# Attention of the second block: one wide row of scores per tile of queries, with one maximum and one exponential

## The chip, the cores and the metric

The kernel runs on one core of one Trainium2 chip. The metric is the device time of one execution in microseconds (us), as the median of the runs shown. The engines are named as the profile names them: PE (matmul; PEld is its weight load), DVE (vector), ACT (scalar), POOL (GpSimd) and SP (which issues DMAs). PSUM is the accumulator memory that PE writes and that DVE and ACT read; it has eight banks of 512 float32 columns.

## The reference, cut to what matters

The program is two blocks, one behind the other. The first is a mixer with a mixture of experts; the second has two layers, and each layer has, beside other branches, an attention of 4 query heads over 2 key heads of width 64. Only the softmax part of this attention is touched:

```python
def one_block(qi):
    sc = jnp.einsum('bqkgd,bskd->bkgqs', qi, k_all, preferred_element_type=jnp.float32)
    p = jax.nn.softmax(sc, axis=-1).astype(v_all.dtype)
    return jnp.einsum('bkgqs,bskd->bqkgd', p, v_all)
```

`k_all` and `v_all` are 256 context tokens and then 1024 latent tokens, so that a row of scores for a latent query has 1280 columns. In the first of the two layers the 256 context queries attend too, to the 256 context tokens alone; in the second layer only the latent queries do.

## The kernel before

The touched code stands in `layer(l)`, which is called twice, for layer 0 and layer 1. By the time it runs, queries and keys lie transposed in SBUF (`qst`, `kst`), values in `vst`. One **job** is one head and 256 queries, that is, two tiles of 128 queries (`qi` = 0 and 1). Layer 0 has 20 jobs (four of them context queries with 256 columns instead of 1280), layer 1 has 16.

Each job has two parts, which are generators:

- `weights(hd, q0, ...)` makes the softmax weights. For each tile of queries PE writes scores in blocks of up to 512 columns (`s`, L1595, two matmuls for each block: high and low part of the keys), each block in a bank of its own out of five. DVE takes a maximum of each block (L1596), then the maximum of those (L1598) and scales it (L1599). ACT takes the exponential of each block into the SBUF tile `E` and sums each (L1601; the sum's read-out is a second row, ACTIVATION_READ_ACCUMULATOR). DVE adds the three sums (L1603) and inverts (L1604); POOL makes a diagonal matrix `dg` of the inverse (L1606).
- `values(hd, q0, ...)` uses them. PE puts the row sums' inverses into the PSUM bank `o` (L1616), transposes `E` in groups of four 128x128 pieces into one of two banks `t` (L1621). Each `t` is split into a high part `et0` and a low part `et1`: three of five by ACT and DVE (L141, L142), two of five by an ACT copy `er` (L1629) and two POOL operations (L1630, L1631). PE multiplies both with the values into `o` (L1637). At the end ACT copies a part of `o` (`pvl`, L1644), DVE adds it and multiplies the gate (`oa`, `gr`, L1645, L1647), POOL finishes (L1648). There is one bank `o`.

PSUM is full: five banks `s`, two `t`, one `o`. The loop at the end of the code interleaves the values of one job with the weights of the next. The final order on each engine is not that of the code: a scheduler sorts the instructions when the program is built, and a tile pool puts a wait before an instruction that overwrites what another engine still reads. Each engine then runs its queue strictly in order.

Of the kernel before, what the change touches and what calls it, by code (L numbers as in the profile page):

```python
# [10 lines left out]
F32 = mybir.dt.float32  # L11
# [3 lines left out]
AF = mybir.ActivationFunctionType  # L15
OP = mybir.AluOpType
AX = mybir.AxisListType
# [3 lines left out]
P = 128  # L21
D = 1024
T = 1024
C = 256
N = T + C
# [97 lines left out]
def build(ctx, tc, A, out):  # L123
# [6 lines left out]
    V, S, G, PE, SY = nc.vector, nc.scalar, nc.gpsimd, nc.tensor, nc.sync  # L130
# [18 lines left out]
    def bank(pool, tag, bufs):  # L149
        return lambda: pool.tile([P, 512], F32, name=tag, tag=tag, bufs=bufs)  # L150

    ident = load(const, A["k_ident"], [P, P], "ident")
# [251 lines left out]
    with ExitStack() as es:  # L404
# [4 lines left out]
        for j in range(4):  # L409
            s = gemv_chunk(pools, A["w_mod"][0], lh, 512 * j)  # L410
            to_columns(pools, s, mod1[:, 4 * j:4 * j + 4, :], col["b_mod"][:, 4 * j:4 * j + 4])
        V.scalar_tensor_tensor(sc1, mod1[:, 8:16, :], 1.0, col["norm1"][:, :, None].to_broadcast([P, 8, 2]),
                               op0=OP.add, op1=OP.mult)
    with ExitStack() as es:
# [4 lines left out]
        ps = es.enter_context(tile_pool(name="ps1", bufs=1, space=PSUM))  # L419
# [57 lines left out]
        for f2 in range(4):  # L477
            wt = wstream(wp, win, 704 + 256 * f2)
            for f in (2 * f2, 2 * f2 + 1):
# [13 lines left out]
                for a, b in ((0, C), (C, N)):  # L493
                    for j in (0, 1, 3, 4):
# [3 lines left out]
                                               op0=OP.mult, op1=OP.add)  # L498
# [75 lines left out]
    with ExitStack() as es:  # L574
        gp = es.enter_context(tile_pool(name="mg", bufs=1, reuse_waits="tile"))
        ps = es.enter_context(tile_pool(name="ps2", bufs=1, space=PSUM))
# [17 lines left out]
        bias = load(gp, A["b_gate"][0].rearrange("(g o) -> g o", o=1), [16, 1], "bias")  # L594
# [50 lines left out]
        for h in range(4):  # L645
            f0, b0 = 10 * h, 64 + 10 * h
            V.tensor_tensor_scan(R[:, 2, f0:f0 + 10], R[:, 0, f0:f0 + 10], R[:, 1, f0:f0 + 10], 0.0,
                                 op0=OP.max, op1=OP.add)
            V.tensor_tensor_scan(R[:, 2, b0 + 1:b0 - 1:-1], R[:, 0, b0 + 1:b0 - 1:-1], R[:, 1, b0 + 1:b0 - 1:-1], 0.0,
                                 op0=OP.max, op1=OP.add)  # L650
# [629 lines left out]
    def layer(l):  # L1280
# [295 lines left out]
        with ExitStack() as es:  # L1576
            ap = es.enter_context(tile_pool(name="ab", bufs=1, side="right", reuse_waits="tile"))
            ps = es.enter_context(tile_pool(name="ps9", bufs=1, space=PSUM, reuse_waits="tile"))
            pt_, po_ = bank(ps, "t", 2), bank(ps, "o", 1)
            def weights(hd, q0, Es, dgs):  # L1580

                kh = hd // 2
                nk = C if q0 < C else N
                kbs = [(k0, min(512, nk - k0)) for k0 in range(0, nk, 512)]
                nb = len(kbs)
                for qi in range(2):
                    sl = slice(q0 + qi * P, q0 + qi * P + P)
                    E = ap.tile([P, N], F32, name="E", bufs=5)
                    mx = ap.tile([P, 4], F32, name="mx", bufs=4)
                    dn = ap.tile([P, 4], F32, name="dn", bufs=4)  # L1590
                    sb = []
                    for b, (k0, n) in enumerate(kbs):
                        sc = ps.tile([P, 512], F32, name="s", tag="s", bufs=5)
                        for x in range(2):
                            PE.matmul(sc[:, :n], qst[:, hd, sl], kst[x][:, kh, k0:k0 + n], start=x == 0, stop=x == 1)  # L1595
                        V.tensor_reduce(mx[:, b:b + 1], sc[:, :n], axis=AX.X, op=OP.max)  # L1596
                        sb.append(sc)
                    V.tensor_reduce(mx[:, 3:4], mx[:, 0:nb], axis=AX.X, op=OP.max)  # L1598
                    V.tensor_scalar(mx[:, 3:4], mx[:, 3:4], -0.125, None, op0=OP.mult)  # L1599
                    for b, (k0, n) in enumerate(kbs):  # L1600
                        S.activation(E[:, k0:k0 + n], sb[b][:, :n], AF.Exp, scale=0.125, bias=mx[:, 3:4],  # L1601
                                     accum_out=dn[:, b:b + 1])
                    V.tensor_reduce(dn[:, 3:4], dn[:, 0:nb], axis=AX.X, op=OP.add)  # L1603
                    V.reciprocal(dn[:, 3:4], dn[:, 3:4])  # L1604
                    dg = ap.tile([P, P], F32, name="dg", bufs=4)
                    G.tensor_scalar(dg, ident, dn[:, 3:4], 1.0, op0=OP.mult, op1=OP.mult)  # L1606
                    Es.append(E)
                    dgs.append(dg)
                    yield
# [158 lines left out]
```

## Time and profile before

| | us |
|---|---|
| median of 3 runs (lowest to highest) | 3309.79 (3307.93 to 3311.59) |
| the profiled execution | 3317.06 |
| its span, first to last instruction | 3315.2 |
| attention of layer 0 in that span, about | 2492 to 2648 |
| attention of layer 1 in that span, about | 3084 to 3221 |
| busy over the span: PE, DVE, ACT, POOL | 3116.6, 2218.9, 1536.9, 642.6 |

The profile names each instruction by its engine, its line and its tiles (`out<-in`). "Busy" of PE has the end of a matmul modelled, so a row of n matmuls is longer than n times their distance; the chain view gives the distance. The granted clock is the share of TensorE's full clock that the chip allowed.

### The profile page before, as it was taken

To read this page: it belongs to the slowest core of one execution; us is meant where nothing else is said; L and a number is where in the kernel's file an instruction comes from. 1 tells how busy PE (TensorE), PEld (TensorE's weight loads), DVE (VectorE), ACT (ScalarE), POOL (GpSimd) and SP (SyncE) were. 2 spreads that over 40 slices of the span, in tenths; PEclk is the share of its full clock that TensorE was granted. 3 is DMA by queue.
4 is the path that set the end of the run, shared out by engine and by line. 5 is a ranking of instruction groups with operands and counts; after the bars stand their busy time and mean duration, and the time that the engine had idled before them with its cause. 6 is when DMAs were issued, how large, how long until landed. Compare 5 with 4: busy or idle time off the path is not lost. (4 is left out here: it accounts for less than half of the span.)

```text
span 3315.2 us, 47729 instructions
## 1 busy us (share of the span) xinstructions
PE 3116.6 (94%) x17089; PEld 2623.6 (79%) x17089; DVE 2218.9 (67%) x4837; ACT 1536.9 (46%) x3076; POOL 642.6 (19%) x852
## 2 busy tenths in 40 slices
PE   7997998999999999959999999899999898999999
PEld 5985876999998888858887777688877787887787
DVE  4485878667666653488999888677427746642773
ACT  4223444555555222217777677621137714212770
POOL 0012322222222000330110010211014501101450
PEclk9998999999999999979999999899999999999999
DMA  8541111000003532459999997433200033111002
GB/s 291 151 121 42 37 43 64 7 15 10 5 11 101 153 113 67 166 205 340 393 386 376 359 355 263 154 109 109 65 29 33 20 123 124 45 48 47 33 28 100
DMA packets 224010, 425.93 MB, mean 128 GB/s; under 512 B 28684, under 2 KB 121468, under 8 KB 223772
## 3 DMA queue, kind: packets, MB, share of 16 engines
q1 hardware_dynamic: 215708, 393.51, 33.7%
q0 software_dynamic: 8064, 29.36, 3.1%
q8 instruction: 135, 2.21, 0.3%
q14 instruction: 103, 0.84, 0.1%
HBM read 379.22 MB, written 43.61 MB: 128 GB/s over the span
## 5 line engine op out<-in xcount | busy, mean ns | idle before, releaser
L145 PE MATMUL acc<-hH,wHL 128*128 128x512 f32 (+1 forms) x1296 | 485.4, 376 | 6.1 <-ACT wHL L141 4.1
L146 PE MATMUL acc<-hL,wHL 128*128 128x512 f32 (+1 forms) x1296 | 483.9, 374 | 0.5 <-DVE hL L142 0.5
L147 PE MATMUL acc<-hH,wHL 128*128 128x512 f32 (+1 forms) x1296 | 482.1, 373 | 0.0
L142 DVE TENSOR_TENSOR ewL<-ewr,ewH 128x1024 fp32r<-128x1024 f32 x320 | 371.7, 1221 | 17.0 <-ACT ewH L141 13.9
L141 ACT ACTIVATE ewH<-ewr 128x1024 fp32r<-128x1024 f32 x320 | 328.5, 1059 | 80.4 <-PE acc L1217 69.4
L145 PEld LDWEIGHTS acc<-hH,wHL 128*128 128x128 f32 x1296 | 244.3, 189 | 55.3 <-ACT wHL L141 7.1
L146 PEld LDWEIGHTS acc<-hL,wHL 128*128 128x128 f32 x1296 | 244.5, 189 | 44.9 <-issue 2.6
L147 PEld LDWEIGHTS acc<-hH,wHL 128*128 128x128 f32 x1296 | 243.9, 189 | 44.3 <-issue 1.6
L142 DVE TENSOR_TENSOR wHL<-wr,wHL 128x512 fp32r<-128x512 f32 (+1 forms) x160 | 111.9, 704 | 224.4 <-ACT wHL L141 223.6
L142 DVE TENSOR_TENSOR et<-t,et 128x512 fp32r<-128x512 f32 x264 | 180.1, 686 | 60.6 <-ACT et L141 59.2
L141 ACT ACTIVATE wHL<-wr 128x512 fp32r<-128x512 f32 (+1 forms) x160 | 101.6, 638 | 254.0 <-PE acc L146 221.6
L141 ACT ACTIVATE et<-t 128x512 fp32r<-128x512 f32 x264 | 156.5, 606 | 133.7 <-PE t L917 113.2
L1217 PE MATMUL acc<-ewH,xTH 128*128 128x512 f32 x512 | 201.7, 394 | 0.2 <-ACT xTH L141 0.2
L1217 PE MATMUL acc<-ewH,xTL 128*128 128x512 f32 x512 | 200.8, 392 | 0.0
L302 DVE SCALAR_TENSOR_TENSOR ga<-gw,lh,ga 128x512 f32<-128x512 f32 x224 | 161.0, 749 | 52.2 <-DMA gw<-in_w_mod_dram 51.0
L183 POOL TENSOR_SCALAR E<-E,sm 128x512 f32<-128x512 f32 (+1 forms) x192 | 117.6, 630 | 326.2 <-ACT E L172 101.2
L1217 PE MATMUL acc<-ewL,xTH 128*128 128x512 f32 x512 | 161.5, 399 | 13.8 <-DVE ewL L142 13.8
L170 DVE TENSOR_REDUCE sm<-s 128x1 f32<-128x512 f32 (+1 forms) x192 | 113.1, 598 | 59.3 <-PE s L901 54.6
L145 PE MATMUL acc<-wHL,hH 128*128 128x256 f32 (+1 forms) x464 | 144.9, 321 | 2.9 <-DVE hH L430 1.3
L146 PE MATMUL acc<-wHL,hH 128*128 128x256 f32 (+1 forms) x464 | 139.8, 307 | 0.0
L1596 DVE TENSOR_REDUCE mx<-s 128x1 f32<-128x512 f32 (+1 forms) x200 | 114.8, 589 | 28.7 <-PE s L1595 27.0
L147 PE MATMUL acc<-wHL,hL 128*128 128x256 f32 (+1 forms) x464 | 130.6, 317 | 2.7 <-DVE hL L1315 2.2
(568 smaller groups left out, 7864.9 us busy)
## 6 DMA issues: line engine op xcount, KB each, us to landing
ewr<-in_w_e_up_dram SPq DMA_DIRECT2D x64, 1024.0 KB
ewr<-in_w_e_gate_dram SPq DMA_DIRECT2D x62, 1024.0 KB
wr<-in_w_in_dram SPq DMA_DIRECT2D x152, 256.0 KB
ewr<-in_w_e_down_dram SPq DMA_DIRECT2D x34, 1024.0 KB
ahead<-in_w_e_down_dram SPq DMA_DIRECT2D x30, 1024.0 KB
gw<-in_w_mod_dram SPq DMA_DIRECT2D x96, 256.0 KB
gw<-in_w_mod_dram SPq DMA_DIRECT2D x32, 512.0 KB
wm<-in_w_mod_dram SPq DMA_DIRECT2D x4, 2048.0 KB
```

The lines of the kernel that those rows point to most:

```text
L141: S.activation(H, src, AF.Copy)
L142: V.tensor_sub(L, src, H)
L145: PE.matmul(o, lh[0], rh[0], start=start, stop=False)
L146: PE.matmul(o, lh[0], rh[1], start=False, stop=False)
L147: PE.matmul(o, lh[1], rh[0], start=False, stop=stop)
L170: V.tensor_reduce(ng[:, b:b + 1], sc, axis=AX.X, op=OP.max)
L183: G.tensor_scalar(E[:, k0:k0 + n], E[:, k0:k0 + n], f[:, b:b + 1], 1.0, op0=OP.mult, op1=OP.mult)
L302: V.scalar_tensor_tensor(acc[x], wk, ck, acc[x], op0=OP.mult, op1=OP.add) if k else
L1217: PE.matmul(pa[:, n], x[:, k], w[:, 512 * n:512 * n + 512], start=k == 0 and x is xT[0] and w is H, stop=k == 7 and w is L)
L1596: V.tensor_reduce(mx[:, b:b + 1], sc[:, :n], axis=AX.X, op=OP.max)
```

## The change

The five banks `s` become one tile `wide_s` of 2 x 1280 columns. The scores of the first query tile of a job lie in columns 0 to 1279 of it (two banks and the first half of the third), those of the second in columns 1280 to 2559 (the second half of the third bank and two more). The matmuls are the same in number and size; the second tile's blocks are now 256, 512, 512 wide, so that none crosses a bank. One maximum and one exponential run over all 1280 columns. The maxima over the three maxima (L1598) and the sum over the three sums (L1603) go. For a context tile the first 256 columns of its half are used.

```diff
--- before.py
+++ after.py
@@ -1577,33 +1577,32 @@
             ap = es.enter_context(tile_pool(name="ab", bufs=1, side="right", reuse_waits="tile"))
             ps = es.enter_context(tile_pool(name="ps9", bufs=1, space=PSUM, reuse_waits="tile"))
             pt_, po_ = bank(ps, "t", 2), bank(ps, "o", 1)
+            wide_s = ps.tile([P, 2, N], F32, name="s", tag="s", bufs=1)
+            wide_s = (wide_s[:, 0], wide_s[:, 1])
+
             def weights(hd, q0, Es, dgs):
 
                 kh = hd // 2
                 nk = C if q0 < C else N
-                kbs = [(k0, min(512, nk - k0)) for k0 in range(0, nk, 512)]
-                nb = len(kbs)
                 for qi in range(2):
                     sl = slice(q0 + qi * P, q0 + qi * P + P)
                     E = ap.tile([P, N], F32, name="E", bufs=5)
-                    mx = ap.tile([P, 4], F32, name="mx", bufs=4)
-                    dn = ap.tile([P, 4], F32, name="dn", bufs=4)
-                    sb = []
-                    for b, (k0, n) in enumerate(kbs):
-                        sc = ps.tile([P, 512], F32, name="s", tag="s", bufs=5)
+                    mx = ap.tile([P, 2], F32, name="mx", bufs=4)
+
+                    if nk == N:
+                        sc = wide_s[qi]
+                        kbs = ((0, 512), (512, 512), (1024, 256)) if qi == 0 else ((0, 256), (256, 512), (768, 512))
+                    else:
+                        sc, kbs = wide_s[qi][:, :C], ((0, C),)
+                    for k0, n in kbs:
                         for x in range(2):
-                            PE.matmul(sc[:, :n], qst[:, hd, sl], kst[x][:, kh, k0:k0 + n], start=x == 0, stop=x == 1)
-                        V.tensor_reduce(mx[:, b:b + 1], sc[:, :n], axis=AX.X, op=OP.max)
-                        sb.append(sc)
-                    V.tensor_reduce(mx[:, 3:4], mx[:, 0:nb], axis=AX.X, op=OP.max)
-                    V.tensor_scalar(mx[:, 3:4], mx[:, 3:4], -0.125, None, op0=OP.mult)
-                    for b, (k0, n) in enumerate(kbs):
-                        S.activation(E[:, k0:k0 + n], sb[b][:, :n], AF.Exp, scale=0.125, bias=mx[:, 3:4],
-                                     accum_out=dn[:, b:b + 1])
-                    V.tensor_reduce(dn[:, 3:4], dn[:, 0:nb], axis=AX.X, op=OP.add)
-                    V.reciprocal(dn[:, 3:4], dn[:, 3:4])
+                            PE.matmul(sc[:, k0:k0 + n], qst[:, hd, sl], kst[x][:, kh, k0:k0 + n], start=x == 0, stop=x == 1)
+                    V.tensor_reduce(mx[:, 0:1], sc, axis=AX.X, op=OP.max)
+                    V.tensor_scalar(mx[:, 0:1], mx[:, 0:1], -0.125, None, op0=OP.mult)
+                    S.activation(E[:, :nk], sc, AF.Exp, scale=0.125, bias=mx[:, 0:1], accum_out=mx[:, 1:2])
+                    V.reciprocal(mx[:, 1:2], mx[:, 1:2])
                     dg = ap.tile([P, P], F32, name="dg", bufs=4)
-                    G.tensor_scalar(dg, ident, dn[:, 3:4], 1.0, op0=OP.mult, op1=OP.mult)
+                    G.tensor_scalar(dg, ident, mx[:, 1:2], 1.0, op0=OP.mult, op1=OP.mult)
                     Es.append(E)
                     dgs.append(dg)
                     yield
```

In the built program the change moves instructions on every engine in both attention stages. In the rows below a name's number tells buffers apart, and `[waits ...]` names the engines whose progress the instruction waits for.

PE before, within the second layer: `s_31075`, `s_31079` and `s_31083` are the three blocks of one query tile, `s_31118` the first block of the next tile, `o`/`et`/`t` belong to the values of earlier jobs.

```order
L1595 MATMUL s_31075<-kst0_28961,qst_28958 128x512 [waits Activation_49]
L1595 MATMUL s_31075<-kst1_28962,qst_28958 128x512
L1637 MATMUL o_30887<-et1_30937,vst_28963 128x256 [waits Pool_49]
...
L1595 MATMUL s_31079<-kst0_28961,qst_28958 128x512 [waits Activation_49]
L1595 MATMUL s_31079<-kst1_28962,qst_28958 128x512
L1621 MATMUL t_31044<-ident_68,E_30863 128x128 [waits Activation_49]
...
L1595 MATMUL s_31083<-kst0_28961,qst_28958 128x256 [waits Activation_49]
L1595 MATMUL s_31083<-kst1_28962,qst_28958 128x256
L1595 MATMUL s_31118<-kst0_28961,qst_28958 128x512 [waits Activation_49]
```

PE now, at a like place: `s_28952` is the wide tile; here its first half is written for the next job. `E_29511` and `E_29584` are the weights of the two query tiles of the job before, `t_29634` the first bank of their transposes. (The rows left out repeat the two above them.)

```order
L1615 MATMUL o_29631<-dg_29523,ones_28608 128x128 [waits DVE_49,Activation_49]
L1599 MATMUL s_28952<-kst0_28610,qst_28607 128x512 [waits Activation_49]
L1599 MATMUL s_28952<-kst1_28611,qst_28607 128x512
...
L1599 MATMUL s_28952<-kst0_28610,qst_28607 128x256
L1599 MATMUL s_28952<-kst1_28611,qst_28607 128x256
L1620 MATMUL t_29634<-ident_68,E_29584 128x128
L1620 MATMUL t_29634<-ident_68,E_29511 128x128
```

What moved: the blocks of one tile, which stood apart with a wait each, stand in one run behind one wait on ACT; and the transposes that read `E_29584`, the newest exponential, come right behind the run without any wait of their own.

ACT before, in the second layer: three exponentials of one tile follow each other, between the copies of `t` and `pvl`.

```order
L141 ACTIVATE et0_31049<-t_31044 128x512 [waits PE_49,Activation_49]
L1629 ACTIVATE er_31064<-t_31057 128x512 [waits PE_49,Activation_49,Pool_49]
L141 ACTIVATE et0_31101<-t_31096 128x512 [waits PE_49,Activation_49]
L1601 ACTIVATE E_31072,dn_31074<-s_31075,mx_31073 128x512 [waits DVE_49]
L1601 ACTIVATE E_31072,dn_31074<-s_31079,mx_31073 128x512
L1601 ACTIVATE E_31072,dn_31074<-s_31083,mx_31073 128x256
L1644 ACTIVATE pvl_31109<-o_31013 64x256 [waits PE_49]
```

ACT now, one whole job from one second-half exponential (`E_29584`) to the next (`E_29690`), with the first-half one (`E_29617`) between them.

```order
L1602 ACTIVATE E_29584,mx_29585<-s_28952,mx_29585 128x1280 [waits DVE_49]
L141 ACTIVATE et0_29639<-t_29634 128x512 [waits PE_49,Activation_49]
L1628 ACTIVATE er_29654<-t_29647 128x512 [waits PE_49,Activation_49,Pool_49]
L141 ACTIVATE et0_29667<-t_29662 128x512 [waits PE_49,Activation_49]
L1602 ACTIVATE E_29617,mx_29618<-s_28952,mx_29618 128x1280 [waits DVE_49]
L1628 ACTIVATE er_29682<-t_29675 128x512 [waits PE_49,Activation_49,Pool_49]
L141 ACTIVATE et0_29709<-t_29704 128x512 [waits PE_49,Activation_49]
L1643 ACTIVATE pvl_29717<-o_29631 64x256 [waits PE_49]
L1602 ACTIVATE E_29690,mx_29691<-s_28952,mx_29691 128x1280 [waits DVE_49]
```

What moved: one exponential stands for three, and between two of them stand two or three copies of `t`, each of which waits for PE.

DVE now, at the same place: `mx_29618` is the maximum for `E_29617`; `et1_29640` is the low part of `t_29634`.

```order
L1603 RECIPROCAL mx_29585<-mx_29585 128x1 [waits Activation_49]
L1600 TENSOR_REDUCE mx_29618<-s_28952 128x1 [waits PE_49,Pool_49]
L142 TENSOR_TENSOR et1_29640<-t_29634,et0_29639 128x512 [waits Activation_49]
L1601 TENSOR_SCALAR mx_29618<-mx_29618 128x1 [waits DVE_49]
L142 TENSOR_TENSOR et1_29668<-t_29662,et0_29667 128x512 [waits Activation_49]
L1603 RECIPROCAL mx_29618<-mx_29618 128x1 [waits Activation_49]
```

What moved: the one maximum of the tile stands alone, and the scaling that the exponential waits for (L1601 now) has a subtraction between it and the maximum.

## Rows read from the trace of the kernel before

**Rows 1.** The page, part 1: busy time of the engines over the span.

```profile
PE 3116.6 (94%) x17089; PEld 2623.6 (79%) x17089; DVE 2218.9 (67%) x4837; ACT 1536.9 (46%) x3076; POOL 642.6 (19%) x852
```

**Rows 2.** Windows: us, busy time (instructions) of each engine, granted clock, DMA share, GB/s.

```profile
3084.00:3221.00 137.00, 126.91 (x886) 112.54 (x886) 106.43 (x302) 110.85 (x291) 78.83 (x107) 0.98 0.02 8
3100.00:3200.00 100.00, 95.61 (x685) 84.61 (x684) 81.05 (x235) 83.66 (x223) 64.84 (x88) 1.00 0.00 1
```

**Rows 3.** Timeline, ACT's L1644: first and last of 20, then of 16 jobs.

```profile
2506.52 0.38 ACT L1644 ACTIVATE pvl<-o 64x256 f32<-64x256 f32 x1
...
2647.34 0.38 ACT L1644 ACTIVATE pvl<-o 64x256 f32<-64x256 f32 x1 [1.44 <-PE o L1637]
...
3100.30 0.38 ACT L1644 ACTIVATE pvl<-o 64x256 f32<-64x256 f32 x1
...
3220.78 0.38 ACT L1644 ACTIVATE pvl<-o 64x256 f32<-64x256 f32 x1 [1.44 <-PE o L1637]
```

**Rows 4.** Groups by shape, 3084 to 3221 us: busy us, mean ns | idle before.

```profile
L1601 ACT ACTIVATE E<-s,mx 128x512 f32<-128x512 f32 x64 | 43.7, 695 | 5.9 <-DVE mx L1599 5.9
L1596 DVE TENSOR_REDUCE mx<-s 128x1 f32<-128x512 f32 x62 | 41.9, 684 | 3.9 <-PE s L1595 3.3
L1631 POOL TENSOR_TENSOR et<-er,et 128x512 fp32r<-128x512 f32 x30 | 38.5, 1285 | 1.8
...
L142 DVE TENSOR_TENSOR et<-t,et 128x512 fp32r<-128x512 f32 x50 | 34.0, 683 | 3.4 <-ACT et L141 3.0
...
L141 ACT ACTIVATE et<-t 128x512 fp32r<-128x512 f32 x50 | 29.6, 605 | 11.2 <-PE t L1621 10.6
...
L1630 POOL TENSOR_SCALAR et<-er 128x512 fp32r<-128x512 f32 x30 | 18.5, 617 | 17.1 <-ACT er L1629 15.5 <-PE o L1637 0.5 <-PE s L1595 0.4
L1629 ACT ACTIVATE er<-t 128x512 f32<-128x512 f32 x30 | 18.0, 601 | 0.7
L1601 ACT ACTIVATE E<-s,mx 128x256 f32<-128x256 f32 x32 | 15.6, 489 | 0.0
...
L1596 DVE TENSOR_REDUCE mx<-s 128x1 f32<-128x256 f32 x31 | 13.1, 422 | 8.9 <-PE s L1595 8.3
...
L1644 ACT ACTIVATE pvl<-o 64x256 f32<-64x256 f32 x16 | 6.1, 379 | 8.2 <-PE o L1637 8.0
```

**Rows 5.** Chain that ended last, the second layer's attention: start us, us, pieces merged.

```profile
3098.37 1.90 ACT E L1601 x6
...
3103.91 0.87 PE t L1621 x8
...
3106.64 0.84 PE o L1637 x7
3108.16 0.93 PE s L1595 x4
```

**Rows 6.** Timeline, 3126 to 3140 us: start us, us, engine, line [idle <-releaser].

```profile
3128.37 0.14 DVE L1599 TENSOR_SCALAR mx<-mx 128x1 f32<-128x1 f32 x1
...
3128.54 0.69 ACT L1601 ACTIVATE E<-s,mx 128x512 f32<-128x512 f32 x1 [0.57 <-DVE mx L1599]
...
3129.13 0.19 ACT L1601 ACTIVATION_READ_ACCUMULATOR E<-s,mx 128x1 f32 x1
...
3130.73 1.41 PE L1595 MATMUL s<-kst,qst 128*128 128x256 f32 x6
...
3137.99 0.23 ACT L1601 ACTIVATION_READ_ACCUMULATOR E<-s,mx 128x1 f32 x1
...
3138.28 0.50 PE L1595 MATMUL s<-kst,qst 128*128 128x256 f32 x2 [0.17 <-ACT E L1601]
```

**Rows 7.** Line L1243: ns min/median/max of an ACT read across two banks.

```profile
L1243 ACT ACTIVATE ea<-acc x16: 1006/1028/1029, 1510.4 to 2041.8; 128x1024 f32<-128x1024 f32 x16
```

**Rows 8.** Windows with a lower granted clock (the column behind POOL).

```profile
300.00:330.00 30.00, 16.15 (x66) 11.16 (x66) 16.19 (x45) 11.14 (x16) 11.76 (x9) 0.64 0.15 57
2060.00:2100.00 40.00, 26.14 (x103) 20.09 (x101) 23.46 (x28) 17.57 (x24) 3.95 (x5) 0.75 0.43 136
```

## The prediction

> **What bounds the kernel now.** I read the page first, then windows of the touched stages, the last-ending chain in them, their groups by shape and single handovers. PE is busy for 94% of the span [rows 1], so time is saved only where PE waits. The two attention stages are the place to look, since the change touches nothing else. In layer 1's PE is busy 126.9 of 137 us, but ACT 110.9 and DVE 106.4 too [rows 2]: three engines are each near full, and the chain passes from one to another (pieces of PE, ACT and, in between, DVE) [rows 5].
>
> Time per job: the last ACT instruction of a job runs at 3100.30 in the first and at 3220.78 in the last of layer 1's 16 jobs [rows 3]: 120.5 us over 15 steps, **8.03 us a job**. In layer 0, 140.8 us go over 19 steps, three of which end a short context job.
>
> What a job costs PE: transposes stand 0.109 apart (8 in 0.87), value matmuls of 256 columns 0.12 (7 in 0.84), score matmuls of 512 columns 0.2325 (4 in 0.93) [rows 5]. A full job has 20, 20 and 8 of these and 4 score matmuls of 256 columns (0.12 each, as the value matmuls): 2.18 + 2.40 + 1.86 + 0.48 = 6.9; four small ones for the diagonals, taken as transposes, make 7.4. So 0.6 us a job is all that shorter work on ACT and DVE could win: 31 steps of full jobs (15 in layer 1, 16 in layer 0) x 0.6 = 19 us.
>
> **What is removed.** ACT: three exponentials of a tile take 1.90 from the first start to the last sum [rows 5]. One of 512 with its sum takes 0.78 (3128.54 to 3129.32) [rows 6]; columns cost 0.206 us per 256 (695 - 489 ns) [rows 4], so 1280 take 0.78 + 3 x 0.206 = **1.40**. DVE: maxima of 684, 684 and 422 ns [rows 4] become one of 684 + 3 x 262 = 1470 ns, **1.47**. The small reductions over three columns go as well; L1599, of the same size, takes 0.14 [rows 6]. That is 0.5 us of ACT and 0.6 of DVE per tile, twice a job. Does an access over more than one bank cost extra? The nearest row says no: ACT reads 1024 columns in two banks in 1028 ns [rows 7], less than twice one of 512. PE's work and the DMAs stay.
>
> **What is added: a wait.** Before, each block of scores had its own bank of five and waited for the exponential that last read that bank. Now, in PE's order, the six matmuls of a tile stand behind one wait on ACT, and the transposes of the newest weights (`E_29584`) follow without a wait. Since they read what that exponential wrote, the wait ahead of the scores must already cover it. The first tile's scores therefore wait for the second tile's exponential of the job before; and those of the second tile for the first's, by the same pattern. The two halves never work at the same time. They share the third bank, and that is where I see the reason. So scores, maximum, scaling and exponential of each tile form one closed chain through the whole stage.
>
> The chain for one tile: from the sum's end (3137.99 + 0.23) to the scores 0.06; six score matmuls with their end 1.41; maximum 1.47; scaling 0.14 and 0.03 on to ACT [rows 6]; exponential 1.40. Sum 4.51 us, **9.0 us a job**, even if nothing ever stands in its way. That is 1.0 more than now.
>
> Things do stand in its way, since each queue is in order. I follow one job of the commonest pattern from the end of the second tile's exponential (time 0), with the durations of [rows 4] and the distances above, 0.05 for a handover, 0.2 for the last result of PE to land (1.41 against 1.17 of distances), and the next instruction on ACT or DVE starting 0.1 before the last one's reported end, as the sum's row does [rows 6].
>
> - PE: scores 0.06 to 1.23, then six transposes to 1.9. ACT copies `t` 1.8 to 2.4 and `er` 2.3 to 2.9 (605 and 601 ns). The next four transposes wait for `er` (their bank): 2.95 to 3.4.
> - DVE: maximum 1.5 to 3.0; the subtraction that stands before the scaling (683 ns) to 3.6; scaling to 3.65. ACT has one more copy ahead (from those transposes, 3.65 to 4.25), so the first tile's exponential runs 4.15 to 5.55.
> - POOL, from `er`: 617 ns to 3.6, 1285 ns to 4.9. PE needs that low part, so it stands until 4.95, then seven value matmuls (0.84) and four transposes (0.44): the second tile's scores start at 6.25 rather than 5.6, and land at 7.65.
> - ACT: `er` 5.5 to 6.1, POOL's two parts after that to 8.1; PE's last eight value matmuls wait for it and land at 9.2; `pvl` (379 ns) to 9.6. DVE: a subtraction to 7.8, maximum 7.75 to 9.2, scaling 9.3. The second exponential stands behind `pvl`: 9.55 to 10.95.
>
> So about **11.0 us a job** in this pattern. In a second pattern, in which the first tile's exponential stands ahead of that third copy, it runs 3.7 to 5.1, the scores follow at once and land at 6.55; maximum to 8.05, a subtraction ahead of the scaling to 8.75, exponential to **10.3**. In PE's order layer 1 has 13 jobs of the first and 2 of the second kind, layer 0 5 and 10, and one more that I count as the second: 18 x (11.0 - 8.03) + 13 x (10.3 - 8.03) = 53.5 + 29.5 = **+83 us**. The context tiles (8) have the same wait; their blocks are short, and I count nothing for them. Upper bound: all of a chain of half a full tile's, 8 x 1.6 = 13 us. Start and end of the stages hold the same instructions; nothing counted.
>
> The profiled execution took 3317.06, 7.3 above the median of the runs shown (0.22%); the sum is +83 against either, so from the median 3309.8 I get **3393 us**.
>
> **A rule weighed.** The order has the wait ahead of all six matmuls of the first tile, the first four of which write banks that the other half doesn't touch. If only the third bank tied the halves, those four (0.93) [rows 5] could run ahead of the wait in every job: 31 x 0.93 = 29 us less, 3364. The order shows the wait ahead of them, so I go by the order. [...]
>
> **Rivals.**
>
> 1. **The bare chain.** Copies, POOL and PE's other work fall into the gaps better than my pass has them, and only the 9.0 decides: 31 x (9.02 - 8.03) = +31, **3341**. For it: DVE and ACT have 0.6 and 0.5 us a tile less to do. Against it: `pvl` and the copies stand ahead of the exponentials in ACT's order, and wait for PE and POOL.
> 2. **A lower clock on top.** PE works 7.4 of 11 us, in pieces with gaps. [...] At 0.83 PE's 7.4 become 8.9; if half of the 1.5 lies on the path, 31 x 0.75 = +23, **3416**; all of it, 3439. [...]
> 3. **Faster.** The exponential is over before PE gets round to the next scores, so that the wait costs nothing and PE alone is left: 7.4 a job, -19 us, **3290**. It decides if the chain is under 3.7 us a tile (half of 7.4): maximum and exponential together would have to take 2.1 instead of 2.87. No row points there; by columns they don't come below 2.87.
> 4. **No change.** The chain comes out at 4.0 a tile, and shorter work pays for the wait: **3310**. It asks for 0.5 us less than the rows give.
> 5. **Only the third bank waits**, as weighed above: **3364**. Against it is the place of the wait in PE's order.
>
> **How the numbers follow.** From no change a measurement of this kernel tells about 0.2%, 6.6 us. Chances: my pass, with its error of some tenths per job (3370 to 3415), 0.55; bare chain 0.17; only the third bank 0.05; lower clock 0.15; no change 0.03; faster 0.05. Slower by over 0.2%: 0.55 + 0.17 + 0.05 + 0.15 = 0.92. The range reaches from the bare chain, 3338, to the lower clock with part of the context tiles' 13 us, 3430. It leaves out no change, faster, and the tails of the others.
>
> **What would show it.** Right: a step of 10.3 to 11.0 us from `pvl` to `pvl`; one exponential of about 1.3 us plus its sum, one maximum of 1.47; PE waiting on "ACT E" before the scores and on POOL's low part; PE's busy share in the stages well under 90%; the two stages together some 80 us longer, and all else as it was. Wrong: scores of one half overlapping the other half's exponential, or a wide maximum or exponential far from 1.47 and 1.40 (my lines by columns failed), or a step at 8 us or less. A granted clock under 1 in the middle of a stage speaks for the second rival.

## The result and the profile after

The changed kernel takes **3433.0 us** (median of 4 runs, 3426.6 to 3433.5) against 3310.7 for the kernel before (4 runs): ratio 1.0361, 95% interval 1.0349 to 1.0373, slower by 122 us. The forecast was 3393 with a range up to 3430. The sign and the serial chain came as forecast; the size lies 3 us above the range.

The profiled execution has a span of 3431.1 us, 115.9 more than before. The sums below are made against that. Line numbers of the touched part have moved: scores are now L1599, the maximum L1600, its scaling L1601, the exponential L1602, `pvl` L1643. First the page's part 1, to set beside [rows 1]:

```profile
PE 3167.7 (92%) x17089; PEld 2647.0 (77%) x17089; DVE 2206.0 (64%) x4565; ACT 1512.0 (44%) x2820; POOL 644.2 (19%) x852
```

ACT and DVE lose 25 and 13 us of busy time. PE's instructions are as many as before, and yet PE is busy 51 us longer. Most of that is not a lower clock: a job had 95.61 / 100 x 8.03 = 7.7 us of busy PE before, at a clock of 1.00 [rows 2], and has 9.27 in the last single step below, at 1.00 as well; over 31 steps that is 49 us. "Busy" has the end of a matmul modelled, and PE's work now stands in more separate pieces; that this makes up the difference is not shown.

The next lines are from the view of one line, the scores: what PE and its weight load waited for there (us, times), first before, then now.

```profile
its engine sat idle before it (us, times) until:
  ACT E L1601: 15.4, 19
```

```profile
its engine sat idle before it (us, times) until:
  ACT E L1602: 84.9, 72
```

The two queues are counted apart, PE 28 times and its weight load 44 times now, so the 72 is not the number of tiles (of which there happen to be 72 too). PE stands only where it comes to the scores before the exponential is over. That the order holds everywhere is seen from the start times: none of the 400 recorded score matmuls starts while an exponential runs, where 179 of 400 do in the kernel before. The groups by shape in layer 1's attention (busy us, mean ns | idle before) show what became of the rows of [rows 4]:

```profile
L1600 DVE TENSOR_REDUCE mx<-s 128x1 f32<-128x1280 f32 x28 | 41.6, 1487 | 23.0 <-PE s L1599 23.0
...
L1602 ACT ACTIVATE E<-s,mx 128x1280 f32<-128x1280 f32 x29 | 38.4, 1325 | 3.5 <-DVE mx L1601 3.2
...
L1602 ACT ACTIVATION_READ_ACCUMULATOR E<-s,mx 128x1 f32 x29 | 5.7, 197 | 0.0
```

The windows below have the same columns as [rows 2]. The first four run from one `pvl` to the next, so each is a job's step; the fifth is all of layer 1's 15 steps, the last all of layer 0's 19.

```profile
3174.10:3186.90 12.80, 10.60 (x56) 8.69 (x56) 6.16 (x12) 5.95 (x10) 5.24 (x7) 0.87 0.01 1
3186.90:3199.26 12.36, 9.39 (x56) 7.42 (x56) 6.29 (x12) 7.30 (x12) 5.28 (x7) 1.00 0.00 0
3199.26:3208.86 9.60, 8.82 (x56) 7.18 (x56) 5.86 (x10) 4.46 (x8) 5.26 (x7) 1.00 0.01 3
3208.86:3220.20 11.34, 9.27 (x56) 7.33 (x56) 6.34 (x13) 5.88 (x10) 5.25 (x7) 1.00 0.00 0
3162.74:3336.68 173.94, 142.39 (x826) 114.48 (x826) 90.78 (x163) 88.28 (x149) 74.71 (x100) 0.95 0.00 1
...
2503.25:2703.19 199.94, 159.24 (x938) 130.37 (x938) 107.06 (x203) 100.78 (x177) 84.79 (x117) 0.93 0.01 2
```

Where the 115.9 us are: layer 1's steps 173.94 against 120.48 [rows 3], +53.5; layer 0's 199.94 against 140.82, +59.1; the stretch between the stages' `pvl` (2703.19 to 3162.74) +6.6; the first `pvl` comes 3.3 earlier; behind the last one both kernels take 94.4. Of the 6.6, 3.1 lie between layer 1's first scores and its first `pvl` (25.3 against 22.2); the rest lies ahead of those scores, and 2.9 of the 3.3 ahead of layer 0's first scores, in code that the change leaves alone.

One job at full clock, in the timeline, PE, DVE and ACT alone:

```profile
3210.49 0.19 ACT L1602 ACTIVATION_READ_ACCUMULATOR E<-s,mx 128x1 f32 x1
...
3210.73 1.43 PE L1599 MATMUL s<-kst,qst 128*128 128x512 f32 x6
...
3212.00 0.82 PE L1620 MATMUL t<-ident,E 128*128 128x128 f32 x6
3212.27 1.49 DVE L1600 TENSOR_REDUCE mx<-s 128x1 f32<-128x1280 f32 x1 [1.39 <-PE s L1599]
...
3214.27 0.14 DVE L1601 TENSOR_SCALAR mx<-mx 128x1 f32<-128x1 f32 x1
...
3214.97 1.32 ACT L1602 ACTIVATE E<-s,mx 128x1280 f32<-128x1280 f32 x1
...
3215.80 1.10 PE L1636 MATMUL o<-et,vst 128*128 128x256 f32 x7 [0.21 <-POOL et L1630]
...
3217.09 1.41 PE L1599 MATMUL s<-kst,qst 128*128 128x256 f32 x6
...
3218.68 1.48 DVE L1600 TENSOR_REDUCE mx<-s 128x1 f32<-128x1280 f32 x1
...
3220.20 0.38 ACT L1643 ACTIVATE pvl<-o 64x256 f32<-64x256 f32 x1 [2.17 <-PE o L1636]
3220.60 1.33 ACT L1602 ACTIVATE E<-s,mx 128x1280 f32<-128x1280 f32 x1
```

Read it as the closed chain: the sum ends at 3210.68, scores start at 3210.73, the maximum at 3212.27, the exponential at 3214.97. The second tile's scores (3217.09) do not wait for ACT, which was done at 3216.38; PE is late there, since its seven value matmuls stood for POOL until 3215.80. The second exponential stands behind `pvl`. That is the course the forecast walked through.

### The profile page after: what moved, and what is told of

Its sections match the earlier page's. It is cut to its first block, busy times and chain, and to the rows that moved or that the text cites. A ratio compares the mean times of both kernels' runs of the same rounds, so it can differ in the third digit from the quotient of the medians.

```text
span 3431.1 us, 47209 instructions
## 1 busy us (share of the span) xinstructions
PE 3167.7 (92%) x17089; PEld 2647.0 (77%) x17089; DVE 2206.0 (64%) x4565; ACT 1512.0 (44%) x2820; POOL 644.2 (19%) x852
## 5 line engine op out<-in xcount | busy, mean ns | idle before, releaser
L1599 PE MATMUL s<-kst,qst 128*128 128x512 f32 (+1 forms) x400 | 110.5, 417 | 40.5 <-ACT E L1602 36.9
L1636 PE MATMUL o<-et,vst 128*128 128x256 f32 x656 | 128.4, 310 | 14.7 <-POOL et L1630 6.3
```

The source lines that it names most:

```text
L1599: PE.matmul(sc[:, k0:k0 + n], qst[:, hd, sl], kst[x][:, kh, k0:k0 + n], start=x == 0, stop=x == 1)
L1636: PE.matmul(pv[:, :256], vst[:, k, kh, 1 - g:3 - g].rearrange("p b e -> p (b e)"), ET[x][:, kk * 256:kk * 256 + 256], start=(k == 0 and x ...
```

## The experiments

Three theories were put against each other. **T**: the scores of a tile are tied to the tile just before, and that tie makes a serial chain. **W**: a wide maximum and a wide exponential cost it by themselves, because no maximum runs beside scores any more. **C**: PE's gaps bring the granted clock down, on top of either.

### Width against tie, cleanly: three kernels with 1024 keys

With 1024 keys a tile of queries needs two banks, so that two tiles fit beside the transposes' two banks with no bank shared. `k1_1024_keys` is the kernel before with fewer keys. `k2_wide_own_tiles` has the wide operations and a score tile for each half:

```diff
+ wide_s = [ps.tile([P, 1024], F32, name=f"s{x}", tag=f"s{x}", bufs=1) for x in range(2)]
...
+ V.tensor_reduce(mx[:, 0:1], sc, axis=AX.X, op=OP.max)
+ S.activation(E[:, :nk], sc, AF.Exp, scale=0.125, bias=mx[:, 0:1], accum_out=mx[:, 1:2])
```

`k3_wide_one_tile` differs from it in two lines:

```diff
- wide_s = [ps.tile([P, 1024], F32, name=f"s{x}", tag=f"s{x}", bufs=1) for x in range(2)]
+ wide_s = ps.tile([P, 2, 1024], F32, name="s", tag="s", bufs=1)
+ wide_s = (wide_s[:, 0], wide_s[:, 1])
```

> Leaves out the last 256 keys for the latent queries (1024 of 1280 keys: scores, exponentials, transposes, values), so its time is to be compared with the two that leave out the same. Otherwise the kernel before: five banks of scores in turn, a maximum and an exponential per 512 columns. A job is a fifth smaller but for the fixed parts: 8.03 x 0.8 = 6.4 to 6.6 us, 31 x 1.5 = -45: about 3265 (3255 to 3290).

> The same 1024 keys as the run with 1024 keys, with one maximum and one exponential of 1024 columns per tile of queries, each half in a tile of two banks of its own, and the transposes with both their banks. A half's scores wait for that half's exponential of the job before. Theory T (the tie costs it): within -15 to +10 us of the narrow kernel with 1024 keys. Theory W (the width costs it): 30 to 60 us above it.

> As the wide kernel with 1024 keys, but both halves lie in one tile of four banks; no bank is shared, two banks for each half. In PE's order every tile's scores wait for the exponential of the tile just before, as in the changed kernel. Theory T: closed chain per tile 0.06 + 1.15 + 1.23 + 0.2 + 1.2 = 3.85, with the queues' delays as in the changed kernel (11.3 against 9.0 bare) 4.8: 9.6 a job against about 6.5, so +70 to +110 us above the wide kernel with tiles of their own. If the shared third bank, and not the shared tile, is what ties: no more than 10 us above it. Theory W: no more than 10 us above it, since the width is the same.

Measured: 3266.0, 3264.5 and **3345.4 us** (against before 0.9842, interval 0.9814 to 0.9869; 0.9836, 0.9808 to 0.9863; 1.0091, 1.0062 to 1.0119). Width costs nothing. One allocation for both halves costs 81 us, with no bank in common. What PE and its weight load, each counted, waited for ahead of the scores, first with two tiles, then with one, and the windows of layer 1's steps of both:

```profile
  ACT E L1601: 28.0, 14
```

```profile
  ACT E L1602: 82.8, 96
```

```profile
3074.90:3172.93 98.03, 91.26 (x636) 80.03 (x634) 68.23 (x143) 68.31 (x128) 73.52 (x98) 1.00 0.01 3
```

```profile
3119.26:3244.80 125.54, 106.94 (x650) 86.27 (x650) 74.77 (x147) 71.48 (x132) 74.53 (x100) 1.00 0.01 5
```

98.0 us become 125.5, and PE's busy share falls from 93 to 85%, at a clock of 1.00 in both: here the tie alone does it. With one tile no score matmul starts while an exponential runs (0 of 272), with two 65 do. In layer 0 (161.5 against 115.1) part of the price is the clock: the steps behind the context jobs there have 0.87. Theory W is out. The bank is out as its necessary cause too: I had named the shared third bank as the reason of the wait; the shared tile is enough.

### Wide rows in tiles of their own, 1280 keys

`x1_own_tiles` gives each half three banks and its own tile; the eight banks then leave one for transposes. `x2_one_t_bank` is the control.

```diff
- pt_, po_ = bank(ps, "t", 2), bank(ps, "o", 1)
+ pt_, po_ = bank(ps, "t", 1), bank(ps, "o", 1)
```

```diff
- wide_s = ps.tile([P, 2, N], F32, name="s", tag="s", bufs=1)
- wide_s = (wide_s[:, 0], wide_s[:, 1])
+ wide_s = [ps.tile([P, 1536], F32, name=f"s{x}", tag=f"s{x}", bufs=1) for x in range(2)]
+ wide_s = [t[:, :N] for t in wide_s]
```

The first diff is in both kernels, the second in `x1_own_tiles` alone, from the changed kernel.

> One maximum and one exponential per tile as in the changed kernel, but each half has a score tile and three banks of its own; for that the transposes have one bank in place of two. The scores of a half then wait for that half's exponential of the job before, two tiles back. Theory T: the chain no longer decides, a job takes what the kernel with one transposition bank and narrow instructions takes, or up to 0.5 us less: within -20 to +10 us of that control. Theory W: at least 40 us above the control, since a wide maximum and a wide exponential still stand one behind the other.

> Control: the kernel before, with one transposition bank in place of two and nothing else. Each group of four transposes then waits for the readers of the group before (about 0.6 to 0.7 us); five groups a job, so up to 5 x 0.7 = 3.5 us a job if nothing covers it, 31 jobs = +108. Both theories: slower than before, 3330 to 3420; it only sets the scale for the kernel with two tiles of their own.

Measured: 3526.9 (ratio 1.0652, 1.0635 to 1.0670) and 3536.6 (1.0662, 1.0639 to 1.0685): 10 us below the control by the medians, with intervals that overlap, as T expects. The control itself I had far too low: one transposition bank costs 223 us, a step in layer 1 then takes 13.9 to 16.4. That stall is so long that it could hide part of a chain, and the granted clock in that stage of the control is 0.84, so this pair says less than the three kernels above.

### The tie without wide operations

`x3_layout_alone` keeps the changed kernel's one tile, but takes maxima and exponentials by block again; `b3_three_banks` is the kernel before with three banks of scores.

```diff
+ for b, (k0, n) in enumerate(kbs):
      for x in range(2):
          PE.matmul(sc[:, k0:k0 + n], qst[:, hd, sl], kst[x][:, kh, k0:k0 + n], start=x == 0, stop=x == 1)
+     V.tensor_reduce(mx[:, b:b + 1], sc[:, k0:k0 + n], axis=AX.X, op=OP.max)
```

```diff
- sc = ps.tile([P, 512], F32, name="s", tag="s", bufs=5)
+ sc = ps.tile([P, 512], F32, name="s", tag="s", bufs=3)
```

> The changed kernel's one tile of five banks, but with three maxima and three exponentials per tile of queries, as before. Theory T (the one shared tile ties each tile's scores to the tile before, whatever the width): the waits are now on single pieces, but on those of the tile just before, so the two halves still take turns; chain per tile 0.06 + 0.47 (first two matmuls) + 1.79 (three maxima) + 0.3 + 0.2 + 0.8 to 1.9 (first to last exponential) = 3.6 to 4.7 us, 7.2 to 9.4 a job bare, and with the queues' delays some 1.5 more: 3340 to 3420. Theory W (the wide instructions cost it, because no maximum runs beside the scores and no transpose beside the exponential, and the layout is harmless): 3310 to 3325, as before.

> The kernel before, with three banks for the scores in place of five: each block of scores waits for the exponential of the third block back, that is the same block of the tile just before. A tie between tiles, but piece by piece and with narrow instructions. Theory T: slower, by the chain per tile of 0.06 + 0.47 + 1.79 + 0.3 + 0.2 + 0.8 = 3.6 us bare and more with the queues: 3340 to 3420, near the kernel that has the layout alone. Theory W: 3310 to 3325.

Measured: 3611.1 (1.0905, 1.0880 to 1.0930) and 3392.1 (1.0230, 1.0202 to 1.0258). Both are slow with narrow instructions, so a tie to the tile just before costs time without any wide operation; with three banks, block by block, it costs 78 us, at steps of 10.3 and 10.9 (one of them in the window below, at a clock of 1.00). But the layout alone costs 298 us, far above my 3340 to 3420. The view of its scores' line, behind the window, shows one reason:

```profile
3165.27:3175.60 10.33, 8.50 (x58) 7.14 (x57) 6.58 (x20) 6.86 (x19) 5.21 (x7) 1.00 0.01 2
```

```profile
  DVE mx L1602: 83.2, 69
  ACT E L1606: 65.0, 99
```

The wait on a maximum was not in my expectation: inside one tile the next block's matmuls wait until the block ahead has been read. In the timeline (PE alone) two matmuls go, then the next two stand for DVE:

```profile
3314.22 1.20 PE L1601 MATMUL s<-kst,qst 128*128 128x512 f32 x2
3316.20 1.22 PE L1601 MATMUL s<-kst,qst 128*128 128x512 f32 x2 [0.78 <-DVE mx L1602]
```

So scores and maxima take turns three times a tile. In the first twelve of layer 1's 15 steps PE is busy only 144.4 of 205.1 us, and the granted clock is 0.70:

```profile
3261.05:3466.14 205.09, 144.44 (x672) 106.28 (x672) 90.44 (x228) 84.81 (x218) 62.93 (x84) 0.70 0.00 1
```

No run tells how the 298 us divide between this wait and the clock. In this layout the change's wide operations do not cost time: with them, and the higher clock that comes with them (0.95 in layer 1), the kernel is 178 us faster than without.

### The clock

`c1_filler` adds eight transposes per full job, whose result the next real ones overwrite:

```diff
+ first = pt_()
+ if nkt > 2:
+     for _ in range(8):
+         PE.transpose(first[:, 0:P], Es[0][:, 0:P], ident)
```

> The changed kernel with eight more transposes per full job, into the bank that the next real transposes overwrite: nothing but work for PE, 8 x 0.109 = 0.87 us at full clock. In PE's order they stand behind the second tile's scores, ahead of the values on which the second exponential waits, so I count them on the path: 31 x 0.87 = +27. In the changed kernel five of 15 steps of layer 1 have a granted clock of 0.86 to 0.87 and take 12.5 to 12.8 us in place of 11.34. Theory C (PE's gaps bring the clock down, and the clock adds about 1.4 us in such a step): with fewer gaps the clock is 1.00 in all steps, which are then alike at 12.2, and the low steps' 5 x 1.4 = 7 in layer 1 and some 5 in layer 0 come back: 3433 + 27 - 12 = 3448. If the gaps are not what lowers it: the low steps stay, at 13.6: 3460.

Measured: 3443.0 (1.0390, 1.0365 to 1.0416). First what the low clock does in the changed kernel. Its five steps of 12.5 to 12.8 us in layer 1 have PE's instructions in the same order as the step of 11.34 above. The timeline of one (PE alone):

```profile
3315.90 2.49 PE L1599 MATMUL s<-kst,qst 128*128 128x512 f32 x6
3318.19 1.39 PE L1620 MATMUL t<-ident,E 128*128 128x128 f32 x6
```

2.49 for what took 1.43, and 1.39 for 0.82. The windows of these pieces in the slow and in the full step:

```profile
3315.90:3319.40 3.50, 3.50 (x12) 3.13 (x13) 1.04 (x2) 0.27 (x1) 0.55 (x2) 0.51 0.00 0
3210.73:3213.04 2.31, 2.31 (x14) 1.94 (x14) 0.92 (x2) 0.45 (x1) 0.55 (x2) 1.00 0.00 0
```

The granted clock is 0.51 over the slow pieces (0.50 from 3316 to 3319 us) and 1.00 over the others; ahead of the slow ones PE had stood 1.36 us for `gr`, with only a pair of matmuls between. The same wait stands ahead of the pieces at full clock, so it is not this one gap alone:

```profile
3210.19 0.46 PE L1615 MATMUL o<-dg,ones 128*128 128x128 f32 x2 [1.36 <-DVE gr L1646]
...
3315.35 0.46 PE L1615 MATMUL o<-dg,ones 128*128 128x128 f32 x2 [1.36 <-DVE gr L1646]
```

With filler, its timeline row, and two windows, a step and all of layer 1:

```profile
3226.88 1.03 PE L1617 MATMUL t<-ident,E 128*128 128x128 f32 x8
```

```profile
3217.40:3229.13 11.73, 9.74 (x64) 8.11 (x64) 6.22 (x12) 5.87 (x11) 5.25 (x7) 1.00 0.01 1
3170.46:3345.36 174.90, 144.83 (x938) 120.19 (x938) 90.75 (x162) 87.84 (x149) 74.47 (x100) 0.99 0.00 1
```

All 14 steps of layer 1 that contain filler are 11.72 to 11.76 us at 1.00; the last step, which has none, is at 0.84. Layer 1 takes 174.9, 1.0 more than without. So theory C holds there: with more work for PE the low clock goes, which five of 15 steps have without it (0.86 to 0.87). In layer 0 the steps behind a context job stay at 0.83 to 0.90, and the layer takes 208.4 in place of 199.9; the 5 us that I expected back there are not seen. The filler cost 0.39 a step and not 0.87, since what stands behind it moved closer together: from the second tile's scores to the last seven values 1.98 us (3217.09 to 3219.07) without, 2.39 (3225.62 to 3228.01) with it. One thing differs beside the filler: the built order has none of the second pattern's pairs left in layer 1. The five low steps were of the first pattern, so the comparison of these stands.

### Layer 0: the context jobs

In the changed kernel the step behind a context job takes 16.2 to 17.2 us:

```profile
2503.25:2519.45 16.20, 12.05 (x64) 9.47 (x64) 7.97 (x14) 7.30 (x12) 5.65 (x8) 0.89 0.00 1
```

`j1_context_first` does the four context jobs at the start; `j2_before_context_first` is the same order in the kernel before.

```diff
- for job in [(hd, q0, [], []) for hd in range(4) for q0 in range(T0, N, 256)] + [None]:
+ for job in [(hd, q0, [], []) for hd, q0 in sorted([(hd, q0) for hd in range(4) for q0 in range(T0, N, 256)], key=lambda t: t[1] >= C)] + [None]:
```

> The changed kernel with layer 0's four context jobs done one after the other at the start, in place of one ahead of each head's four full jobs. In the changed kernel's profile the step behind a context job takes 16.2 to 17.2 us (four of them), since the full job there has only a short job's values to work beside; the other full steps of layer 0 average 10.3. Theory L (this link is what the forecast left out in layer 0): only one such link is left, 3 x (16.5 - 11.0) = 16 us less, some of it given back by context jobs that stand beside each other: 3415 to 3425. Against it: the link's time is the first full job's chain and falls due anyway: 3428 to 3436.

> Control: the kernel before, with the same order of jobs as the run with the context jobs first. Its steps behind a context job take 8.7, 7.2 and 8.3 us, no more than the others, so nothing is to be won: 3305 to 3318.

Measured: 3435.5 (1.0364, 1.0338 to 1.0390) and 3312.5 (0.9996, 0.9982 to 1.0009). The order changes nothing in either, so theory L fell. One link of 16.47 is left in the trace, but the steps of 8.3 ahead of a context job, where a full job's values run beside a short job's weights, are gone too: no full step is under 9.4. In ACT's order the step behind a context job holds three wide exponentials and the next step only one, which fits the other side of my expectation, that the link's time is the chain's and falls due anyway.

So the four jobs were left out, in both kernels and in the one with filler:

```diff
- for job in [(hd, q0, [], []) for hd in range(4) for q0 in range(T0, N, 256)] + [None]:
+ for job in [(hd, q0, [], []) for hd in range(4) for q0 in range(C, N, 256)] + [None]:
```

> Leaves out the attention of layer 0's 256 context queries (four jobs; zeros stand in their place), in the kernel before. Both theories: layer 0's stage then has 15 steps of some 8.0 us, as layer 1's 120.5, in place of 140.8: 3286 to 3294.

> The changed kernel without the same four context jobs, to be set against the kernel before without them. Theory P (layer 0's extra loss is the price of its full jobs, which each cost 3.6 us more, as in layer 1, and not 2.5 as I had them): layer 0's 15 steps take some 174 us, as layer 1's, and the difference of the two kernels is 2 x 53.5 + 3 = 110. Theory X (the context jobs cost the rest, and the full jobs are priced right): layer 0's 15 steps take 120.5 + 38 = 158, and the difference is 53.5 + 38 + 3 = 95.

> The changed kernel without the four context jobs and with eight transposes of filler per full job. Theory C (the low clock comes from PE's gaps): all steps of both layers 11.72 to 11.76 us at 1.00, layer 0's stage 175 as layer 1's, so that what the run without filler has above 11.34 a step in layer 0 is its low clock. Else low steps stay, above 12 us.

Measured: 3304.0 (0.9971, 0.9960 to 0.9982), 3410.3 (1.0297, 1.0280 to 1.0315) and 3420.4 (1.0322, 1.0304 to 1.0339). The first misses its range: layer 0's steps shrink to 120.9 as expected, but the first `pvl` comes 7.6 later, at 2514.07. The changed kernel is 106 us slower than it, of which layer 0's 15 steps give 49.2 (170.1 against 120.9). The windows of layer 0's steps, before, changed, and changed with filler:

```profile
2514.07:2634.95 120.88, 115.15 (x821) 101.37 (x819) 95.97 (x273) 97.72 (x260) 74.08 (x100) 1.00 0.01 1
```

```profile
2518.26:2688.37 170.11, 141.32 (x826) 112.89 (x826) 90.64 (x162) 86.52 (x148) 74.46 (x100) 0.96 0.00 1
...
3144.23:3312.95 168.72, 138.84 (x826) 110.25 (x826) 90.73 (x162) 86.42 (x148) 74.47 (x100) 0.98 0.00 1
```

```profile
2516.94:2692.01 175.07, 144.69 (x938) 120.10 (x938) 90.62 (x162) 87.93 (x150) 74.65 (x100) 0.99 0.00 1
```

Both theories had a part. Without the context jobs the full jobs of layer 0 take as long as those of layer 1 (170.1 and 168.7): 49.2 more than before over 15 steps, where I had 39.8 over 16. With them layer 0 costs 59.1. Of the 9.9 between, 49.2 / 15 = 3.3 are the sixteenth full step, and 6.6 come with the context jobs. This splits totals and not steps, since the built order differs: layer 0 has two steps of the second pattern without the context jobs and ten with them. The filler makes all full steps but the last alike, 11.71 to 11.76, in both layers: theory C again. Without it three steps of layer 0 are low (12.60, 12.72, 12.72, against 11.34), 4 us.

### A version that might beat both

`x4_1024_and_256` has one maximum and one exponential of 1024 columns (two tiles of two banks in turn) and one of 256 in the fifth bank; `x5_1024_256_first` has `j1`'s order as well.

```diff
+ parts = [(0, 256)] if nk == C else [(0, 256), (256, 1024)]
...
+ if n == 256:
+     sc = ps.tile([P, 512], F32, name="s", tag="s", bufs=1)
+ else:
+     sc = ps.tile([P, 1024], F32, name="sw", tag="sw", bufs=2)
```

> Each tile of queries has one maximum and one exponential of 1024 columns in two banks, with two such buffers in turn, and one of 256 columns in the fifth bank; the small three-column steps stay. No bank or tile is shared by two halves but the 256 one, whose exponential comes first. ACT has about 0.2 us and DVE about 0.1 us a tile less to do than before. Theory T: the tie is gone but for the 256 piece, 3290 to 3330. Theory W: the wide pieces delay the chain by one 512 maximum (0.68) and one 512 exponential (0.78) a tile, some 1 to 2 us a job: 3340 to 3380.

> A version that might beat both: the kernel with a 1024-wide and a 256-wide maximum and exponential (3314, no different from before), with the context jobs first as in the two runs above. Its layer 0 has a step of 12.8 us at the start, behind the first context job, and 8.3 to 9.2 behind the others. Expected 3300 to 3316; below 3304 it would be a gain that can be told from no change.

Measured: 3314.1 (1.0005, 0.9996 to 1.0015) and 3316.0 (1.0008, 0.9995 to 1.0022). Neither can be told from the kernel before. All of layer 1's steps in the first:

```profile
3097.98:3214.61 116.63, 112.80 (x804) 99.50 (x802) 92.14 (x235) 88.67 (x197) 72.63 (x97) 1.00 0.00 1
```

PE is busy 97% here. This execution is 3.9 us shorter than [rows 3] in this stage; the medians show nothing of it. The 256 columns have one buffer here, so that tiles take turns in one bank after all, and the total shows no loss; what that costs by itself was not measured.

## Why the forecast was right and wrong

- **The wait.** Right: no tile's scores start before the exponential of the tile ahead is over (0 of 400 matmuls). **Its reason** was wrong. I saw it in the third bank; one tile for both halves is enough (81 us with no bank shared). In the changed kernel both are shared, and a kernel with the bank alone shared and wide rows was not tried: two tiles of 1280 columns take three banks each. The rule that I weighed, a wait for the shared bank alone, would be the smaller guard: this program's goes by tile (with no bank shared, `k3_wide_one_tile` has 0 of 272 score matmuls beside an exponential), and the price that follows is the tile's.
- **Durations.** Right. Maximum 1487 ns against 1.47 us, exponential with its sum 1.42 (3220.60 to 3222.02) against 1.40, over 2.5 banks with no extra cost.
- **The failed step: what a job costs.** I had 11.0 and 10.3 us by pattern, at full clock. Measured mean of a step: 173.94 / 15 = 11.6 in layer 1. Three things are in it.
- *First pattern.* 11.34 at full clock. From the end of the sum at 3210.68: POOL's low part lets PE's values go at 5.12 (I had 4.95), second scores at 6.41 (6.25), `pvl` at 9.52 (9.22), second exponential from 9.92 (9.55). Some tenths, gathered on the way.
- *Second pattern.* It comes in pairs, 12.36 + 9.60 and 12.36 + 9.50, so with the first-pattern job of a pair at 11.34 the second-pattern one costs 10.62 and 10.52, where I had 10.3.
- *Clock.* A third of layer 1's steps lie at 12.71 on average in place of 11.34: 6.8 us. I had this as a rival with a chance of 0.15, as if it took my pass's place; it comes on top of it. That is why the range was too low as well: its end, 3430, leaves out the rival's own upper figure, 3439, and without layer 1's 6.8 alone the time would lie inside it (3433.0 - 6.8 = 3426). The 0.83 in that rival was my estimate, and no run shows the changed kernel's stages at it: they came at 0.95 (layer 1) and 0.93 (layer 0), with single steps at 0.70 to 1.00; the 0.64 and 0.75 of [rows 8] are from other stages.
- **Layer 1's sum.** Forecast 13 x 2.97 + 2 x 2.27 = 43.2, measured 53.5. The 10.3 missing: clock 6.8; ten first-pattern steps at 0.34, 3.4; the two pairs 1.2; less 1.2 for the last step, 9.85, which has no weights beside it.
- **Layer 0's sum.** Forecast 5 x 2.97 + 11 x 2.27 = 39.8, measured 59.1. Of the 19.3 missing, 12.7 are the price of full jobs: 16 x 3.28 = 52.5, by the runs without the context jobs, where I took 11 of 16 for the second pattern at full clock. Three low steps in those runs are 4 us of it. The other 6.6 come with the context jobs, which I counted as nothing while giving them an upper bound of 13. The bound held; the choice of its lower end had no row behind it. The steps behind a context job are at 0.70 to 0.90 in the changed kernel, so a part of the 6.6 is clock; how much, no run shows.
- **Start and end.** Counted as nothing; 6.6 - 3.3 = 3.3 us; 3.1 of them are in layer 1's first job, whose weights have no values beside them, and the rest is what is left of shifts in untouched code.

Together 83 + 10.3 + 19.3 + 3.3 = 115.9, the difference of the spans; the medians lie 122 apart because the profiled execution of the kernel before was 6.4 above its median.

Of the rivals, the bare chain did not come (9.0 a job; 11.6 measured on average in layer 1), faster and no change are out, and with the third bank alone I had the wrong object.

## What to carry to other kernels

Before laying two tiles of work side by side in one PSUM allocation, ask whose readers guard it: here the same wide operations cost nothing in two allocations (3264.5 against 3266.0) and 81 us in one. Price such a chain by walking through each engine's queue, and then once more with PE's pieces behind a standing wait at the lower clock, here 3.50 us at 0.51 for 2.31 at 1.00. If a layout serialises blocks anyway, fewer and wider operations are the better ones in it (3433 against 3611).

## What the runs showed of the hardware

- Work that is thrown away need not cost its length: 0.87 us of filler per job cost 0.39 a step in layer 1 and kept PE at a granted clock of 1.00 in the 14 steps that have it. It does not pay in this kernel as a whole (3443 against 3433 us).
- A step's own instructions do not decide its clock: within one execution, steps with the same order on PE have 1.00 and take 11.34 us, or 0.87 and take 12.80. What decides which steps fall stays open. (Layer 1 has five low steps in the changed kernel and two in the one without context jobs, but its built order differs there too.)
- A second transposition bank is worth 223 us to this kernel; a part of that is the clock, which is 0.84 in layer 1 without it.
- An ACT read and a DVE maximum over 2.5 banks cost what their columns say: 1325 and 1487 ns for 1280, against 1313 and 1470 worked out from 512 and 256 columns [rows 4].
